# A decoder trunk with expert layers: two rows of scheduling constants and one more group of experts ahead of the gates

## The chip, the cores and the metric

The kernel runs on one core of a Trainium2 chip. The metric is the device time of one execution in microseconds (us), the median of several runs. Beside it there is one execution taken with the hardware profiler. The engines are called as in the profile: PE (TensorE, matrix multiply), DVE (VectorE), ACT (ScalarE), POOL (GpSimd), SP (SyncE, which here only issues transfers). Each works through its own instructions in their order and waits for the others by semaphores. The 16 DMA engines are shared by all queues.

## The reference, cut to what matters

Two layers, each a sequence mixer and then a PEER expert layer; 512 tokens of width 1024, float32. The expert layer is what the change concerns:

```
def block(xt):                                  # PEER, per token t and head h (8 heads)
    q = (xt @ w_q).reshape(T, 8, 2, 128)
    s = einsum('thpd,hpkd->thpk', q, sub_keys)  # scores against 2 x 128 keys
    s_top, i_top = top_k(s, 16)
    cand, cand_id = all sums of the two halves, i0 * 128 + i1
    best, pos = top_k(cand, 16); eid = cand_id[pos]; gate = softmax(best)
    act = gelu(einsum('td,thkd->thk', xt, u_tab[eid]))
    return einsum('thk,thkd->td', gate * act, v_tab[eid])
```

There are 16384 experts, each a row of `u_tab` and of `v_tab`; a token uses 8 x 16 = 128 of them.

## The kernel before

Products are in three float32r passes: an operand is split into a high part (ACT, `hi`, L172) and a low part (DVE, `lo`, L173). `stream` loads 128 x 1024 floats (512 KB, `raw`, five buffers, SP's queue) and splits them into one of six pairs of buffers. A block of 128 experts needs its `u` block for the first product (24 matmuls, L188 to L190, into `pA` or `pC`) and its `v` block for the second (18 matmuls, L1137).

An expert layer has these stages:

- *Routing* (`route_topk`). The query projection comes in four chunks of two heads. For each chunk `c` and each block `tb` of 128 tokens, `steps` finds the top 16 of four key sets on DVE, one set a step (L867 to L871); `choose` combines the halves, for the first 128 tokens chunk by chunk, for the others at the end.
- *The first 64 tokens* take their `u` rows by gather. When a chunk's experts are chosen, ACT copies the indices (`ids`, L91), POOL issues 16 gathers (`urow`, L744, eight buffers), and DVE takes 16 dots (L108), whose place among the steps is set by `DOTS[c][tb]`. After them `weigh` multiplies the gates by GELU of the dots; then POOL issues 32 adds (`gz<-gate`, L130) of gate weights into the DRAM tensor `gz`, each an indirect transfer of one number for each of 128 partitions. How many adds are issued where is set by `ADDS[c]`: the first number ahead of `choose`, the second behind it, the third (chunk 0) after a later step. POOL's queue is in order, so gathers wait for the adds ahead of them. Adds of one head wait for the landing of those of the head before.
- *Gates* (`route_gates`): for tokens 128 to 383, one slice of 32 tokens after another, one-hot products on PE give the dense gate weights, which go to DRAM (`gd<-gbuf`, L939).
- *Lookahead* (`lookahead`): beside routing and gates PE takes the first product of the first `NLA` groups of four blocks, for tokens 64 to 383. The results `ge` are spilled to DRAM (`sp`, L767), the last two groups stay. It is advanced by credits that routing and gates hand out; what is left when they end follows behind them.
- *Experts* (`experts`): groups in an order that spreads the "fresh" ones (not taken ahead) among the spilled ones. For each group `fetch` reads back gates (`gt<-gd`, `gt<-gz`) and `ge`; DVE and ACT make `ch` and `cl` from them, PE takes the second product, and, six blocks ahead, the first product of fresh blocks. The first group is fresh and the two after it are the kept ones. Beside it the last 128 tokens are done entirely by gather, in 128 rounds (POOL rows from u and v, L991; DVE dot L1003 and accumulation L1016), paced by `used`: a spilled block counts 1, a fresh one 2, and 140 iterations are spread over the total times 1.02.

The order on each engine is set when the kernel is built, by a scheduler with estimated times that starts from the program's order.

Of the kernel before, what the change touches and what calls it, by code (L numbers as in the profile page):

```python
# [37 lines left out]
GQ = 8  # L38
LAG = GQ + 4
NSD = TD // 32  # L40
NLA = 24
NSZ = 4
KEEP = 2
ROT = 3
# [1 line left out]
QS = 8  # L46
Y2 = 1.45
YA = 2.3
DOTS = ((0, 2, 2, 0), (0, 0, 1, 2), (1, 0, 1, 2), (1, 0, 2, 2))
ADDS = ((0, 0, 16), (4, 12), (6, 26), (0, 64))  # L50
YB = (1.4, 1.4, 1.4, 4.0)
AHEAD = 6
TAIL = 4
# [92 lines left out]
class Kern:  # L146
# [547 lines left out]
    def peer(self, layer, xT, hs, out):  # L694
        nc, tc, io = self.nc, self.tc, self.io
        gd = self.dram.tile([NG, P, NSD - NSZ, NB, 32], F32, name="gd%d" % layer, tag="gd%d" % layer)
        sp = self.dram.tile([NLA, P, NB, TN], F32, name="sp%d" % layer, tag="sp%d" % layer)
        with tc.tile_pool(name="pe", bufs=1) as pe:
# [60 lines left out]
    def lookahead(self, layer, xT, sp):  # L759
        for g in range(NLA):  # L760
            ge = self.pe.tile([P, NB, TN], F32, name="ge", tag="ge", bufs=3)
            for b in range(NB):
                self.mm1(layer, g * NB + b, xT, ge[:, b, :], b % 2 == 1)
                if g >= NLA - KEEP:
                    self.kept[g] = ge
                elif b == NB - 1:
                    self.nc.sync.dma_start(out=sp[g], in_=ge)  # L767
                yield

    def route_topk(self, layer, xT, kT, gz):  # L770
        nc, tc, io = self.nc, self.tc, self.io
        with tc.tile_pool(name="rt", bufs=1) as rt, tc.tile_pool(name="rt2", bufs=2) as rt2, \
# [72 lines left out]
            def scores(tb):  # L845
                ps = self.psB.tile([P, 512], F32, name="pB", tag="pB")
                for i in range(4):
                    nc.tensor.matmul(ps[:, i * P:(i + 1) * P], qs[i][:, tb * P:(tb + 1) * P], keys[:, i, :],
                                     start=True, stop=True)
                return ps  # L850
# [8 lines left out]
            def top16(c, tb, ps):  # L859
                ixs = rs2.tile([P, 4, 16], U32, name="ix", tag="ix", bufs=2)  # L860
                for i in range(4):
                    hp = c * 4 + i
                    sc = ps[:, i * P:(i + 1) * P]
                    mx = stop[:, tb, hp, :]
                    ix = ixs[:, i, :]
                    s2 = rs2.tile([P, P], F32, name="s2", tag="s2")
                    nc.vector.max(out=mx[:, 0:8], in_=sc)  # L867
                    nc.vector.max_index(out=ix[:, 0:8], in_max=mx[:, 0:8], in_values=sc)
                    nc.vector.match_replace(out=s2, in_to_replace=mx[:, 0:8], in_values=sc, imm_value=NEG)
                    nc.vector.max(out=mx[:, 8:16], in_=s2)  # L870
                    yield nc.vector.max_index(out=ix[:, 8:16], in_max=mx[:, 8:16], in_values=s2).ins  # L871
                nc.vector.tensor_copy(itop[:, tb, c * 4:c * 4 + 4, :], ixs)
# [3 lines left out]
            def steps(c, tb, ps, cost, early=0):  # L876
                for i, top in enumerate(top16(c, tb, ps)):
                    if early == "w" and c < 3:
                        w0.append(self.stream(wq[c + 1, i]))
                    with tc.issue_after(top):  # L880
                        gz.dots(self, DOTS[c][tb])
                    yield cost

            for c in range(4):
                yield from steps(c, 0, scores(0), YA)
                if c > 1:
                    gz.weigh(self, rs2)
                gz.add(self, ADDS[c][0])
                yield from choose(0, c * 2, 2)
                gz.add(self, ADDS[c][1])  # L890
                yield from steps(c, 1, scores(1), YA, "w")
                late = [scores(tb) for tb in (2, 3)]
                if c < 3:
                    self.w0, w0 = w0, []
                    keys = project(c + 1)
                for tb in (2, 3):
                    yield from steps(c, tb, late[tb - 2], YB[c])
                    if c == 0 and tb == 2:
                        gz.weigh(self, rs2)
                        gz.add(self, ADDS[c][2])  # L900
            gz.weigh(self, rs2)
# [117 lines left out]
    def experts(self, layer, xT, hs, gd, gz, sp, norm):  # L1019
        nc, tc, io = self.nc, self.tc, self.io  # L1020
        with tc.tile_pool(name="ex", bufs=2) as ex, tc.tile_pool(name="ga", bufs=2) as ga:
# [4 lines left out]
            rounds = self.gather_rounds(layer, (self.eid, self.gate3, self.x3, hs[3]), ga)  # L1026
            total = NLA * NB * 1.0 + (NE - NLA * NB) * 2.0
            done, used = 0, 0.0
            ges = {}
            kept = list(self.kept)  # L1030
            fresh, old = list(range(NLA, NG)), [g for g in range(NLA) if g not in kept]
            fresh = fresh[ROT:] + fresh[:ROT]
# [8 lines left out]
            def fetch(n):  # L1041
# [7 lines left out]
                q = nc.scalar if n > 1 else nc.sync  # L1049
                if g < NLA and g not in kept:  # L1050
                    q.dma_start(out=ge, in_=sp[g])
# [218 lines left out]
```

## Time and profile before

| | |
|---|---|
| median of 3 runs | 2786.56 us (2786.25 to 2786.89) |
| profiled execution | 2787.97 us, its span 2786.1 us |
| mean granted PE clock | 0.984 |
| PE busy | 2681.8 us (96%) |
| DVE busy | 2418.5 us (87%) |
| POOL busy | 1423.1 us (51%) |
| moved by DMA | 830.56 MB, mean 298 GB/s |

In layer 0 the routing with its gathers and adds runs from about 170 to 580 us of the span, the gates to 673, the experts to 1339. In layer 1 the same stages end at about 2020, 2115 and 2776. Timeline rows give start, duration, engine, line, operation, and in brackets the idle time before and what ended it. Rows of waits give the sum, the number and the longest. Rows of windows give busy time and count of PE, PE's weight loads, DVE, ACT and POOL, then the granted PE clock, the DMA share and GB/s. Single matmuls overlap: the spacing of their starts counts, not their length.

### The profile page before, as it was taken

The numbers are of one execution on the slowest core, as the hardware profiler recorded it, in microseconds if no ns is written. First come the engines' busy times: TensorE is split into PE (matmuls) and PEld (weight loads), VectorE is DVE, ScalarE is ACT, GpSimd is POOL, SyncE is SP. The second block draws the span as 40 slices with busy tenths as digits, with TensorE's granted clock in tenths as the row PEclk, the third lists the DMA queues.
The fourth block names the chain that finished last, engine by engine and source line by source line (L and its number), as shares of the span: only waits on it lengthen the run. The fifth ranks groups of instructions, "written<-read, shape, count | busy, mean of one in ns | idle before, by whom it ended". The sixth has DMA issues, their size and how long they took to land. (4 is left out here: it accounts for less than half of the span.)

```text
span 2786.1 us, 41803 instructions
## 1 busy us (share of the span) xinstructions
PE 2681.8 (96%) x15314; PEld 2375.7 (85%) x15314; DVE 2418.5 (87%) x4684; ACT 1093.1 (39%) x1539; POOL 1423.1 (51%) x929
## 2 busy tenths in 40 slices
PE   9999997998999999999999999997998999999998
PEld 7898997997887888888788899997997888888887
DVE  6678887997799999999798678897997899999999
ACT  3343332565333333333334343342654333333332
POOL 0006778781466666565000026778862556666663
PEclk9999998999999999999999999998999999999999
DMA  6357888799999999999322557888799999999995
GB/s 230 123 201 257 267 270 247 218 250 313 353 408 409 414 412 413 410 402 371 104 78 78 201 182 226 260 274 272 195 285 329 366 418 413 410 408 413 413 415 216
DMA packets 330414, 830.56 MB, mean 298 GB/s; under 512 B 63456, under 2 KB 129504, under 8 KB 330208
## 3 DMA queue, kind: packets, MB, share of 16 engines
q1 hardware_dynamic: 177248, 415.08, 42.0%
q0 software_dynamic: 129344, 336.78, 34.0%
q10 hardware_dynamic: 23616, 76.03, 6.9%
q8 instruction: 120, 1.97, 0.3%
q14 instruction: 86, 0.70, 0.1%
HBM read 746.38 MB, written 81.40 MB: 297 GB/s over the span
## 5 line engine op out<-in xcount | busy, mean ns | idle before, releaser
L172 ACT CAST hi<-raw 128x1024 fp32r<-128x1024 f32 (+1 forms) x609 | 637.8, 1051 | 1107.2 <-DMA raw<-in_peer_v 349.9
L173 DVE TENSOR_TENSOR lo<-raw,hi 128x1024 fp32r<-128x1024 f32 (+1 forms) x609 | 732.8, 1213 | 96.8 <-ACT hi L172 93.6
L190 PE MATMUL pA<-xThi,lo 128*128 128x320 f32 (+2 forms) x1712 | 560.4, 327 | 37.1 <-DVE lo L173 37.1
L991 POOL DMA_INDIRECT row<-in_v,eid x256 | 384.5, 1502 | 374.8 <-DVE av L1003 279.8
L130 POOL DMA_INDIRECT gz<-gate,idx x256 | 491.5, 1920 | 147.4 <-issue 78.9
L188 PE MATMUL pA<-xThi,hi 128*128 128x320 f32 (+2 forms) x1712 | 561.6, 328 | 0.2 <-ACT hi L172 0.2
L189 PE MATMUL pA<-xTlo,hi 128*128 128x320 f32 (+2 forms) x1712 | 559.5, 327 | 0.4 <-DVE xTlo L173 0.4
L991 POOL DMA_INDIRECT row<-in_u,eid x256 | 379.6, 1483 | 106.5 <-issue 69.5
L190 PEld LDWEIGHTS pA<-xThi,lo 128*128 128x128 f32 x1712 | 323.2, 189 | 53.1 <-DVE lo L173 38.6
L1016 DVE SCALAR_TENSOR_TENSOR h<-row,cf,h 128x1024 f32<-128x1024 f32 x256 | 327.8, 1280 | 22.3 <-DMA row<-in_v,eid 20.7
L188 PEld LDWEIGHTS pA<-xThi,hi 128*128 128x128 f32 x1712 | 323.2, 189 | 16.0 <-ACT hi L172 0.7
L189 PEld LDWEIGHTS pA<-xTlo,hi 128*128 128x128 f32 x1712 | 323.2, 189 | 16.0 <-DVE xTlo L173 0.7
L1003 DVE CUSTOM_DVE_ANT_0 row<-row,x 128x1024 f32<-128x1024 f32 x256 | 310.8, 1216 | 13.5 <-DMA row<-in_u,eid 13.1
L1137 PE MATMUL pB<-hi,ch 128*128 128x512 f32 x768 | 301.6, 393 | 20.9 <-ACT ch L1086 20.9
L1137 PE MATMUL pB<-lo,ch 128*128 128x512 f32 x768 | 303.9, 396 | 16.6 <-DVE lo L173 15.1
L1137 PE MATMUL pB<-hi,cl 128*128 128x512 f32 x768 | 301.2, 392 | 3.8 <-DVE cl L1093 3.8
L1137 PE MATMUL pC<-hi,ch 128*128 128x512 f32 x768 | 301.4, 392 | 0.0
L1137 PE MATMUL pC<-lo,ch 128*128 128x512 f32 x768 | 301.0, 392 | 0.0
L1137 PE MATMUL pC<-hi,cl 128*128 128x512 f32 x768 | 300.7, 392 | 0.0
L744 POOL DMA_INDIRECT urow<-in_u,ids x128 | 157.2, 1228 | 221.1 <-ACT ids L91 173.3
L190 PE MATMUL pC<-xThi,lo 128*128 128x320 f32 x768 | 240.0, 312 | 11.6 <-DVE lo L173 11.6
L188 PE MATMUL pC<-xThi,hi 128*128 128x320 f32 x768 | 240.8, 314 | 0.0
(280 smaller groups left out, 4571.5 us busy)
## 6 DMA issues: line engine op xcount, KB each, us to landing
raw<-in_peer_ut SPq DMA_DIRECT2D x256, 512.0 KB
raw<-in_peer_v SPq DMA_DIRECT2D x256, 512.0 KB
gd<-gbuf SPq DMA_DIRECT2D x16, 2048.0 KB
gt<-gd ACTq DMA_DIRECT2D x60, 512.0 KB
sp<-ge SPq DMA_DIRECT2D x44, 640.0 KB
ge<-sp ACTq DMA_DIRECT2D x44, 640.0 KB
raw<-in_peer_w_q SPq DMA_DIRECT2D x32, 512.0 KB
gz<-zero SPq DMA_DIRECT2D x64, 256.0 KB
```

What stands on the lines that cost most here:

```text
L130: d = nc.gpsimd.indirect_dma_start(out=flat, out_offset=bass.IndirectOffsetOnAxis(ap=self.idx[c][:, col], axis=0), in_=gate[:, col], in_of ...
L172: self.nc.scalar.copy(hi, src)
L173: return self.nc.vector.tensor_tensor(lo, src, hi.bitcast(F32), ALU.subtract)
L188: nc.tensor.matmul(ps, ah, bh, start=(first and i == 0), stop=False)
L189: nc.tensor.matmul(ps, ah, bl, start=False, stop=False)
L190: nc.tensor.matmul(ps, al, bh, start=False, stop=(last and i == n - 1))
L744: d = self.nc.gpsimd.indirect_dma_start(out=t, out_offset=None, in_=self.io["u%d" % layer], in_offset=bass.IndirectOffsetOnAxis(ap=ids[:, ...
L991: nc.gpsimd.indirect_dma_start(out=t, out_offset=None, in_=io[name], in_offset=bass.IndirectOffsetOnAxis(ap=at, axis=0))
L1003: dot = nc.vector.tensor_tensor_reduce(ur, ur, x, 1.0, 0.0, ALU.mult, ALU.add, av[:, k:k + 1])
L1016: nc.vector.scalar_tensor_tensor(acc, vr, c, acc, ALU.mult, ALU.add)
L1137: nc.tensor.matmul(acc[hf], a[:, ts], b[:, hf * 512:(hf + 1) * 512], start=first and i == 0, stop=last and i == 2)
```

## The change

Three constants and the indexing of one of them; the arithmetic and the number of instructions of each kind of work stay, but for one more group spilled and read back in each layer. `DOTS` now has a number for each of the four steps, the same as before except for chunk 0, whose 16 dots are 0, 1, 2, 2 and then 3, 3, 3, 2 instead of 2 in each of eight steps. `ADDS` moves adds: 18 instead of 20 ahead of the second chunk's gathers, 14 instead of 18 between the second's and the third's, 17 instead of 26 between the third's and the fourth's, and 79 instead of 64 behind the fourth's. `NLA` goes from 24 to 25 groups.

```diff
-NLA = 24
+NLA = 25
...
-DOTS = ((0, 2, 2, 0), (0, 0, 1, 2), (1, 0, 1, 2), (1, 0, 2, 2))
-ADDS = ((0, 0, 16), (4, 12), (6, 26), (0, 64))
+DOTS = (((0,) * 4, (0, 1, 2, 2), (3, 3, 3, 2), (0,) * 4), ((0,) * 4, (0,) * 4, (1,) * 4, (2,) * 4),
+        ((1,) * 4, (0,) * 4, (1,) * 4, (2,) * 4), ((1,) * 4, (0,) * 4, (2,) * 4, (2,) * 4))
+ADDS = ((0, 0, 16), (2, 14), (0, 17), (0, 128))
...
-                        gz.dots(self, DOTS[c][tb])
+                        gz.dots(self, DOTS[c][tb][i])
```

Line numbers behind the constants are one higher after the change.

The first place is POOL's queue in layer 0, from the adds of chunk 0 on (`gate_1408` to `gate_1411` are the gates of the four chunks; `urow` are a chunk's 16 gathers in four rows). Before:

```order
L130 DMA gz_1418<-gate_1408,idx_1412 2097152x1 x20
...
L744 DMA urow_2759<-in_u,ids 128x1024
L130 DMA gz_1418<-gate_1408,idx_1412 2097152x1 x12
L130 DMA gz_1418<-gate_1409,idx_1413 2097152x1 x6
...
L744 DMA urow_3587<-in_u,ids 128x1024
L130 DMA gz_1418<-gate_1409,idx_1413 2097152x1 x26
...
L744 DMA urow_4390<-in_u,ids 128x1024
L130 DMA gz_1418<-gate_1410,idx_1414 2097152x1 x32
L130 DMA gz_1418<-gate_1411,idx_1415 2097152x1 x32
```

And after the change:

```order
L131 DMA gz_1418<-gate_1408,idx_1412 2097152x1 x18
...
L745 DMA urow_2757<-in_u,ids 128x1024
L131 DMA gz_1418<-gate_1408,idx_1412 2097152x1 x14
...
L745 DMA urow_3581<-in_u,ids 128x1024
L131 DMA gz_1418<-gate_1409,idx_1413 2097152x1 x17
...
L745 DMA urow_4375<-in_u,ids 128x1024
L131 DMA gz_1418<-gate_1409,idx_1413 2097152x1 x15
L131 DMA gz_1418<-gate_1410,idx_1414 2097152x1 x32
L131 DMA gz_1418<-gate_1411,idx_1415 2097152x1 x32
```

Between the third and the fourth chunk's gathers 17 adds are left of 26, and 15 adds of the second chunk now follow the last gathers, ahead of the 64.

The second place is DVE in layer 0 at the first chunk's dots (two rows L108 a dot; the `lo` row is a split of a streamed block). Before:

```order
L173 TENSOR_TENSOR lo<-raw,hi 128x1024
L108 ISA urow,avu<-urow,xx 128x1024
L108 ISA avu 128x1
L108 ISA urow,avu<-urow,xx 128x1024
L108 ISA avu 128x1
L870 MAX stop<-s_2116 128x8
L173 TENSOR_TENSOR lo<-raw,hi 128x1024
L108 ISA urow,avu<-urow,xx 128x1024
L108 ISA avu 128x1
L108 ISA urow,avu<-urow,xx 128x1024
L108 ISA avu 128x1
L871 MAX_INDEX ix<-stop,s_2116 128x8
```

And after:

```order
L174 TENSOR_TENSOR lo<-raw,hi 128x1024
L109 ISA urow,avu<-urow,xx 128x1024
L109 ISA avu 128x1
L109 ISA urow,avu<-urow,xx 128x1024
L109 ISA avu 128x1
L871 MAX stop<-s_2113 128x8
L174 TENSOR_TENSOR lo<-raw,hi 128x1024
L109 ISA urow,avu<-urow,xx 128x1024
L109 ISA avu 128x1
L872 MAX_INDEX ix<-stop,s_2113 128x8
L109 ISA urow,avu<-urow,xx 128x1024
L109 ISA avu 128x1
```

The first two dots and the split behind them stand where they stood; from the fourth dot on they come later.

The third place is SP's queue at the end of the gates in layer 0 (`gd<-gbuf` writes a gate slice, `sp<-ge` spills a group, `gt<-gd` reads the first gates back). Before:

```order
L767 DMA sp_1025<-ge 128x1280
L178 DMA raw<-in_peer_ut 128x1024
L178 DMA raw<-in_peer_v 128x1024
L939 DMA gd_1024<-gbuf 128x32x128
L178 DMA raw<-in_peer_v 128x1024 x2
L939 DMA gd_1024<-gbuf 128x32x128
L178 DMA raw<-in_peer_v 128x1024 x2
L939 DMA gd_1024<-gbuf 128x32x128
L178 DMA raw<-in_peer_v 128x1024
L178 DMA raw<-in_peer_ut 128x1024
L939 DMA gd_1024<-gbuf 128x32x128
```

And after:

```order
L179 DMA raw<-in_peer_ut 128x1024 x2
L940 DMA gd_1024<-gbuf 128x32x128
L768 DMA sp_1025<-ge 128x1280
L179 DMA raw<-in_peer_ut 128x1024
L179 DMA raw<-in_peer_v 128x1024
L940 DMA gd_1024<-gbuf 128x32x128
L179 DMA raw<-in_peer_v 128x1024 x2
L940 DMA gd_1024<-gbuf 128x32x128
L179 DMA raw<-in_peer_v 128x1024 x2
L1054 DMA gt<-gd_1024 128x1024 x2
```

Four more `u` blocks are loaded ahead of the first `v` block, so that two gate writes instead of four come behind it. On PE 167 matmuls of the first product stand between the last gate product and the first of the second product, instead of 71: seven blocks instead of three.

## The prediction

> **What bounds the kernel now.** I read the engines' shares first, then who waits for whom on the TensorE (PE), then the time order around its long waits, then the stage windows.
>
> ```profile
> PE 2681.8 (96%) x15314; PEld 2375.7 (85%) x15314; DVE 2418.5 (87%) x4684; ACT 1093.1 (39%) x1539; POOL 1423.1 (51%) x929
> PE pA L190 <- DVE lo L173: 37.1, 6, 17.9
> PE pB L1137 <- ACT ch L1086: 20.9, 2, 10.8
> PE pB L1137 <- DVE lo L173: 15.1, 13, 3.6
> PE pC L190 <- DVE lo L173: 11.6, 4, 4.8
> DVE urow L108 <- DMA urow<-in_u,ids: 76.4, 19, 17.7
> ```
>
> PE is the bound: 96% busy, and nearly all of its idle time is in its four rows here; the fifth is DVE's wait behind two of them. So the change is worth what it takes from them and from the slow clock behind them, less what it adds. Each sits at one place per layer.
>
> **The long wait (37.1 us): the fourth chunk's gathers.** Rows of layer 0 in order of time, then of layer 1; the last two are windows (PE, PEld, DVE, ACT, POOL busy, granted clock, DMA share, GB/s).
>
> ```profile
> 392.63 2.63 POOL L130 DMA_INDIRECT gz<-gate,idx  x1 [0.30 <-issue]
> 427.99 0.42 ACT L91 COPY ids<-eu 64x16 int32<-64x16 int32 x2 [0.30 <-DVE s L869]
> 437.26 0.28 DVE L871 FIND_INDEX8 ix<-stop,s 128x8 uint32<-128x128 f32 x1
> 449.06 1.55 POOL L130 DMA_INDIRECT gz<-gate,idx  x1 [0.30 <-issue]
> 450.91 1.00 POOL L744 DMA_INDIRECT urow<-in_u,ids  x1 [0.30 <-issue]
> 455.15 1.23 DVE L108 CUSTOM_DVE_ANT_0 urow<-urow,xx 128x1024 f32<-128x1024 f32 x1 [17.61 <-DMA urow<-in_u,ids]
> 470.80 0.63 PE L190 MATMUL pA<-xThi,lo 128*128 128x320 f32 x1 [17.94 <-DVE lo L173]
> 1870.61 0.42 ACT L91 COPY ids<-eu 64x16 int32<-64x16 int32 x2 [0.30 <-DVE eu L89]
> 1893.54 1.00 POOL L744 DMA_INDIRECT urow<-in_u,ids  x1 [0.30 <-issue]
> 1897.86 1.23 DVE L108 CUSTOM_DVE_ANT_0 urow<-urow,xx 128x1024 f32<-128x1024 f32 x1 [17.70 <-DMA urow<-in_u,ids]
> 455.00:470.00 15.00, 0.00 (x0) 0.00 (x0) 13.65 (x44) 0.00 (x0) 12.26 (x10) 0.51 0.95 339
> 470.00:480.00 10.00, 9.20 (x47) 9.21 (x48) 10.00 (x28) 1.31 (x2) 8.21 (x6) 0.71 0.94 347
> ```
>
> The indices are ready at 428.4, but POOL works through 26 adds (392.63 to 450.6, 2.23 us each) and starts the gathers 22.5 us later. DVE comes to the first dot at 437.5, stands 17.6 us, and the splits queued behind it (lo, L173) starve PE. Then PE runs at half clock for some us.
>
> **The other waits.** First the earlier chunks, with the first chunk's dots last; then the start of the expert stage.
>
> ```profile
> 356.35 0.42 ACT L91 COPY ids<-eu 64x16 int32<-64x16 int32 x2 [0.30 <-DVE s L869]
> 367.29 1.00 POOL L744 DMA_INDIRECT urow<-in_u,ids  x1 [0.30 <-issue]
> 371.47 1.22 DVE L108 CUSTOM_DVE_ANT_0 urow<-urow,xx 128x1024 f32<-128x1024 f32 x1 [7.84 <-DMA urow<-in_u,ids]
> 301.30 1.23 DVE L108 CUSTOM_DVE_ANT_0 urow<-urow,xx 128x1024 f32<-128x1024 f32 x1 [4.19 <-DMA urow<-in_u,ids]
> 217.60 1.22 DVE L108 CUSTOM_DVE_ANT_0 urow<-urow,xx 128x1024 f32<-128x1024 f32 x1 [2.78 <-DMA urow<-in_u,ids]
> 220.91 1.23 DVE L108 CUSTOM_DVE_ANT_0 urow<-urow,xx 128x1024 f32<-128x1024 f32 x1 [2.07 <-DMA urow<-in_u,ids]
> 223.53 0.64 PE L190 MATMUL pC<-xThi,lo 128*128 128x320 f32 x1 [4.79 <-DVE lo L173]
> 674.01 0.38 SPq L939 DMA_DIRECT2D gd<-gbuf  x1
> 684.55 0.80 SPq L1053 DMA_DIRECT2D gt<-gd  x2
> 694.48 0.79 PE L1137 MATMUL pB<-hi,ch 128*128 128x512 f32 x1 [10.81 <-ACT ch L1086]
> 698.61 0.79 PE L1137 MATMUL pB<-hi,cl 128*128 128x512 f32 x1 [2.06 <-DVE cl L1093]
> 2136.20 0.80 PE L1137 MATMUL pB<-hi,ch 128*128 128x512 f32 x1 [10.06 <-ACT ch L1086]
> 694.00:705.00 11.00, 8.46 (x20) 6.21 (x21) 8.49 (x14) 2.20 (x4) 5.04 (x4) 0.52 1.02 419
> ```
>
> At the start of the experts the last gate slice goes to DRAM at 674.0, has landed at 684.5, is read back, weighed and split; PE, out of blocks at 683.7, idles 10.8 us and crawls at clock 0.52 until 705. Last, the expert stage itself: single matmuls for their spacing, and two windows.
>
> ```profile
> 782.04 0.40 PE L1137 MATMUL pC<-hi,ch 128*128 128x512 f32 x1
> 786.13 0.39 PE L1137 MATMUL pC<-hi,ch 128*128 128x512 f32 x1
> 822.11 0.30 PE L188 MATMUL pA<-xThi,hi 128*128 128x320 f32 x1
> 824.31 0.31 PE L188 MATMUL pA<-xThi,hi 128*128 128x320 f32 x1
> 960.00:1060.00 100.00, 98.65 (x465) 82.79 (x464) 94.33 (x112) 34.37 (x40) 63.25 (x42) 1.00 1.02 412
> 684.00:1320.00 636.00, 615.05 (x2904) 519.63 (x2905) 577.87 (x677) 218.87 (x261) 383.81 (x258) 0.98 1.01 401
> ```
>
> 18 matmuls of 512 columns take 4.09 us, so 0.227 each and 4.09 a block of the second product; 15 of 320 columns take 2.20, so 0.147 each and 3.52 a block of the first. The DMA engines are full (share 1.02 at 412 GB/s): PE and DMA are both at their limit here, and 15.1 us of PE waits (two layers) are the DMA's share.
>
> **The parts and their costs.**
>
> *Fewer adds ahead of the gathers.* Six adds go from before the third chunk's gathers to behind them, and fifteen stand behind the fourth chunk's 16 gathers that stood before; two move behind the second chunk's. Layer 0 on POOL: the second chunk's gathers start some 3.7 us sooner (two adds of 1.85, the step from 449.06 to 450.91), which covers nearly all of the 4.19; the third's at the indices, 356.8 instead of 367.3, so that data lands near 361 and the dot wanted at 363.6 (371.47 less 7.84) does not wait. The 16 gathers took 25 us, so the 17 adds run from about 383 at 2.23, to 421, with the wait between two heads perhaps 424. That is ahead of 428.4, so the fourth chunk's gathers start at the indices, land 4.2 us later (450.91 to 455.15), at 433, and DVE comes at 437.5: no stall, 4 us to spare. In layer 1 the indices are ready at 1871.0 and DVE comes at 1880.2 (1897.86 less 17.70).
> PE gains the 17.94 and the slow clock (470 to 480: 47 matmuls where 10/0.147 = 68 fit, 3.1 us), 21 us. DVE's order at this place is unchanged: eight dots and four top-16 searches still stand between two splits, and PE's stock runs out about when the next split now comes, so I leave 1 us: 20 us a layer, 40 in all. The smaller waits on earlier chunks (11.6 less 4.79 here and about as much in layer 1: 2.2) go too: **42 us**.
> Who pays: 79 adds now follow the last gathers instead of 64. The gathers end 24.0 us after they start (450.91 to 474.89), now at 452; by the two rows at the slower rival an add takes 2.44 us with waits, and 452 + 79 x 2.44 is 645. They must have been issued by 658 (there). Covered, at nothing.
>
> *First chunk's dots later.* On DVE the first two dots stand where they stood (they wait 2.78 and 2.07), and the split behind them, which PE waits for, keeps its place. Only the dots after it move, where PE waits for nothing. Gain 0; bounds -2 (later splits sooner) to +2 (three dots in a row) for both layers.
>
> *25 groups.* Four u blocks a layer go ahead: 4 x 3.52 = 14.1 us of PE work in the hole, with their splits and GELUs, which idle DVE and ACT take. On SP four u loads go ahead of the v loads; the read of gt waits for the landing as before. By 705 PE had done 20 matmuls of the second product; now it ends the blocks at 683.7 + 14.1 = 697.8 and runs on at full clock, 32 by 705: 14.1 + 12 x 0.227 = 16.8 us ahead (layer 1, whose wait is 0.75 shorter, 16). One more group is spilled (SP's queue) and read back (ACT's), 0.66 MB each way, written where PE isn't waiting for DMA.
> But the expert stage loses 14.1 us of PE time and hardly any bytes. A block of a spilled group needs v 0.524, a quarter of gt and ge 0.360, and 140/(160 x 1.02) = 0.858 gather rounds of 1.049 MB: 1.784 MB in 4.09 us, 436 GB/s. A fresh block: 3.045 MB in 7.61 us, 400. A period of 4 fresh and 12.6 spilled blocks: 34.6 MB, 84.0 us at 412 GB/s against 81.9 of PE, 2.1 us over, seven times. Now rounds are 0.880, and a period has 15.3 spilled blocks: 40.1 MB, 97.3 us against 93.2, 4.1 over, six times. The stage pays 24.6 instead of 14.7, **10 us a layer** of the 16. Ends: nothing given back (33 gained in all), everything (0). I take 16.8 + 16 - 20 = **13 us**, since the share 1.02 stands in nearly every window.
>
> The Trainium skill (DMA: Bandwidth & Descriptors, Specifications) puts the ceiling of the 16 DMA engines at 435 GB/s and the HBM's share of one core at about 358. The trace holds 412 over 100 us, so the lower figure does not bind here, and no window shows the upper. By 435 a new period takes 92 us, under PE's 93.2, nothing is given back, and the sum would be 75 us.
>
> Sum: 42 + 0 + 13 = 55 us. The profiled execution took 2787.97 (span 2786.1), 1.4 above the runs' median of 2786.56; so 2733 beside the profile, **2732** as a median.
>
> **Rivals.**
> *Nothing given back* (10%): buffers carry the spilled stretches over the fresh ones. For it: PE's explicit waits there are only 7.5 us a layer. Against: share 1.02. Gain 42 + 33: 2712.
> *All given back* (10%): the expert stage is DMA's alone, and four prefetched v blocks fewer make up for the four u loads. Gain 42: 2744.
> *The gathers stay late* (7%): 17 adds hit the indices' time if they take over 45/17 = 2.65 us each instead of 2.23, for instance beside the denser traffic. At 3.2 they are 9 us late a layer: about 2750.
> *Slower* (4%): the adds' tail. PE now has blocks until about 676 (gates end 21 sooner, 24.6 us of blocks behind), and from the read of gt to the second product went 14 us (684.55 to 698.61); so the last add must have landed by 662.
>
> ```profile
> 474.89 1.95 POOL L130 DMA_INDIRECT gz<-gate,idx  x1 [0.30 <-issue]
> 629.18 1.98 POOL L130 DMA_INDIRECT gz<-gate,idx  x1 [0.30 <-issue]
> ```
>
> 64 adds took 156.3 us, 2.44 each. An add takes about 4 us to land if it is like a gather (450.91 to 455.15), so 658 is the last issue. At (658 - 452)/79 = 2.61 each they begin to hold the experts; the gain is gone at 27 us a layer more, 2.95 each, and at 3.1 the kernel takes 2810. Against: the 64 already ran beside four of the eight gate slices (629.18 lies 45 us ahead of the last one's write) and kept to 2.44.
> *No change* (2%): DVE, busy throughout 455 to 480, absorbs it; but its own stall goes with PE's.
>
> **How the numbers follow.** The likeliest case has 67%, own range 2722 to 2742. The range takes in all given back and most of nothing given back, and the late gathers' edge: 2714 to 2750. A difference under 0.2%, some 5.6 us, cannot be told from none: faster 0.94, same 0.02, slower 0.04.
>
> **What would show it.** Right: DVE's waits for urow fall from 76.4 us to under 20, those of the first chunk staying; the wait of 17.9 is gone and no PE clock near 0.5 is left in the routing but for the first chunk's; PE goes from first to second product with under 2 us between. PE's waits for lo in the expert stage grow from 15 to some 35 us. Wrong: the fourth chunk's first gather later than its indices, or the read of gz later than that of gd.

## The result, and the profile after

The changed kernel takes 2747.67 us (median of 4 runs, 2743.87 to 2748.59); the kernel before, run beside it, 2786.4. The ratio is 0.986 (95% interval 0.9843 to 0.9877): 39 us faster, where 55 were forecast, 2714 to 2750 was the range and 2722 to 2742 that of the likeliest case. The profiled execution took 2748.59 (span 2746.7).

First the engines and who waits for whom, as before the change (line numbers are one higher).

```profile
PE 2679.3 (98%) x15314; PEld 2374.9 (86%) x15314; DVE 2419.7 (88%) x4684; ACT 1093.3 (40%) x1539; POOL 1427.3 (52%) x929
PE pB L1138 <- DVE lo L174: 26.9, 15, 3.2
DVE urow L109 <- DMA urow<-in_u,ids: 21.4, 18, 2.9
PE pC L191 <- DVE lo L174: 10.8, 6, 4.3
PE pB L1138 <- ACT ch L1087: 9.4, 2, 5.3
PE pA L191 <- DVE lo L174: 4.1, 7, 1.0
```

The 37.1 us behind the fourth chunk have become 4.1. The wait at the start of the experts fell only from 20.9 to 9.4, and the waits for `lo` in the expert stage grew from 15.1 to 26.9. Where in the span this lies is read from two marks in each layer: the last gate product and the last matmul of the second product (rows of lines: count, ns, first and last start). First before, then after.

```profile
L934 PE MATMUL pC<-og,oh x64: 217/218/220, 586.8 to 673.0; 128*128 128x128 f16 x64
L1137 PE MATMUL pC<-hi,cl x384: 388/389/628, 699.2 to 1338.9; 128*128 128x512 f32 x192
L934 PE MATMUL pC<-og,oh x64: 217/218/219, 2029.3 to 2115.5; 128*128 128x128 f16 x64
L1137 PE MATMUL pC<-hi,cl x384: 388/389/628, 2140.6 to 2775.6; 128*128 128x512 f32 x192
```

```profile
L935 PE MATMUL pC<-og,oh x64: 218/218/220, 570.7 to 656.8; 128*128 128x128 f16 x64
L1138 PE MATMUL pC<-hi,cl x384: 388/389/628, 689.2 to 1318.4; 128*128 128x512 f32 x192
L935 PE MATMUL pC<-og,oh x64: 217/218/220, 1990.1 to 2076.2; 128*128 128x128 f16 x64
L1138 PE MATMUL pC<-hi,cl x384: 387/389/632, 2107.4 to 2735.0; 128*128 128x512 f32 x192
```

Up to the gates' end the layers became 16.2 us (673.0 to 656.8) and 18.8 us shorter (2115.5 - 1338.9 = 776.6, now 757.8): 35 where the adds' term had 42. The expert stages became 4.3 (665.9 to 661.6) and 1.3 us shorter (660.1 to 658.8): 5.6 where the groups' term had 13.

**The fourth chunk.** Indices, POOL's adds and first gather, PE's waits, and a window (busy times, then clock, DMA share, GB/s), layer 0 after the change:

```profile
425.86 0.42 ACT L92 COPY ids<-eu 64x16 int32<-64x16 int32 x2 [0.30 <-DVE eu L90]
426.86 1.54 POOL L131 DMA_INDIRECT gz<-gate,idx  x1 [6.34 <-DVE iy L103]
428.71 1.71 POOL L745 DMA_INDIRECT urow<-in_u,ids  x1 [0.31 <-issue]
454.66 0.41 PE L191 MATMUL pA<-xThi,lo 128*128 128x320 f32 x1 [0.96 <-DVE lo L174]
459.27 0.41 PE L191 MATMUL pC<-xThi,lo 128*128 128x320 f32 x1 [0.82 <-DVE lo L174]
463.88 0.42 PE L191 MATMUL pA<-xThi,lo 128*128 128x320 f32 x1 [0.83 <-DVE lo L174]
455.00:480.00 25.00, 23.35 (x156) 22.59 (x155) 24.93 (x90) 7.96 (x14) 21.65 (x12) 1.00 0.98 301
```

The stall is gone and PE keeps its full clock, but the gathers start 2.4 us after the indices are copied (428.71 against 425.86 + 0.42). The 17th add is the first of its head; it stood 6.34 us, and the gathers stood behind it. The row names `iy`, which belongs to the fourth chunk's indices and which this add, one of the second chunk's, does not read. What the program makes the add wait for is the landing of the head before, and other first adds stand as long (5.80 us at 1914.29, ended by `DMA gz<-gate`). PE's waits here sum to 2.6 us.

**The start of the experts.** Last add, the reads of the gates (SP's in one row and POOL's in two are those of the first two groups), DVE's weighing and PE's first second product in layer 0, then DVE's first weighing and PE's first second product in layer 1:

```profile
661.77 2.48 POOL L131 DMA_INDIRECT gz<-gate,idx  x1 [0.30 <-issue]
669.42 0.80 SPq L1054 DMA_DIRECT2D gt<-gd  x2
670.73 0.62 POOL L142 DMA_DIRECT2D gt<-gz  x1 [6.47 <-DMA raw<-in_peer_v]
672.67 0.61 POOL L142 DMA_DIRECT2D gt<-gz  x1
682.15 0.82 DVE L1083 TENSOR_TENSOR gt<-gt,ge 128x640 f32<-128x640 f32 x1 [12.28 <-DMA raw<-in_peer_ut]
685.16 0.82 DVE L1083 TENSOR_TENSOR gt<-gt,ge 128x640 f32<-128x640 f32 x1
686.90 0.80 PE L1138 MATMUL pB<-hi,ch 128*128 128x512 f32 x1 [5.29 <-ACT ch L1087]
2100.36 0.82 DVE L1083 TENSOR_TENSOR gt<-gt,ge 128x640 f32<-128x640 f32 x1 [11.10 <-DMA gt<-gz]
2105.11 0.80 PE L1138 MATMUL pB<-hi,ch 128*128 128x512 f32 x1 [4.11 <-ACT ch L1087]
```

DVE's first weighing waits 12.28 us, then two splits run, then the second weighing, and only then does ACT make `ch`. (Layer 0's row names a streamed block as what ended the wait; layer 1's names the read of `gz`.) The first weighing began 12.7 us after the first read (669.42 to 682.15), and PE followed 4.75 us later. Before the change it began 8.2 us after that read (684.55), PE 1.75 us later:

```profile
692.73 1.62 DVE L1082 TENSOR_TENSOR gt<-gt,ge 128x640 f32<-128x640 f32 x2 [6.88 <-DMA gt<-gz]
```
DVE's order in the built program tells why (the numbers tell buffers apart): `gt_7622` holds the gates of the second group in the experts' order (one that was kept), `gt_7619` those of the first.

```
L174 TENSOR_TENSOR lo_7785<-raw_7782,hi_7784 128x1024
L1083 TENSOR_TENSOR gt_7622<-gt_7622,ge_7194 128x10x64
L174 TENSOR_TENSOR lo_7842<-raw_7839,hi_7841 128x1024
L174 TENSOR_TENSOR lo_7854<-raw_7851,hi_7853 128x1024
L1083 TENSOR_TENSOR gt_7619<-gt_7619,ge_7618 128x10x64
```

Before the change both weighings of the first group came first. With 25 groups the scheduler puts one of the kept group, whose `ge` has long been there, ahead; why it does so now was not tested. That group's gates are read second on both queues (POOL's read at 672.67 against 670.73), and DVE takes its instructions in order, so the first group's weighing stands behind a read that was queued later.

### The profile page after: what moved, and what is told of

It is laid out like the page before. It is cut to its first block, busy times and chain, and to the rows that moved or that the text cites. A ratio compares the mean times of both kernels' runs of the same rounds, so it can differ in the third digit from the quotient of the medians.

```text
span 2746.7 us, 41827 instructions
## 1 busy us (share of the span) xinstructions
PE 2679.3 (98%) x15314; PEld 2374.9 (86%) x15314; DVE 2419.7 (88%) x4684; ACT 1093.3 (40%) x1539; POOL 1427.3 (52%) x929
## 4 chain that ended last, share of the span: by engine, by line
PE 50%; DVE 15%; issue 14%; DMA 11%; POOL 8%; ACT 1%; SPq 0%; DVEq 0%; POOLq 0%; ACTq 0%
PE pA L191 9%; PE pA L190 8%; PE pA L189 8%; POOL row L992 7%; PE pB L1138 5%; DMA row<-in_v,eid 5%; PE pC L1138 5%; DVE lo L174 4%; DMA raw<-in_peer_v 3%; PE pC L191 3%; PE pC L189 3%; PE pC L190 3%; DVE h L1017 2%; DVE row L1004 2%; DMA urow<-in_u,ids 1%
## 5 line engine op out<-in xcount | busy, mean ns | idle before, releaser
L131 POOL DMA_INDIRECT gz<-gate,idx x256 | 505.7, 1975 | 165.7 <-issue 72.5
L992 POOL DMA_INDIRECT row<-in_v,eid x256 | 367.0, 1434 | 359.5 <-DVE av L1004 262.9
L191 PE MATMUL pA<-xThi,lo 128*128 128x320 f32 (+2 forms) x1680 | 548.8, 327 | 4.1 <-DVE lo L174 4.1
L189 PE MATMUL pA<-xThi,hi 128*128 128x320 f32 (+2 forms) x1680 | 550.5, 328 | 0.8 <-ACT hi L173 0.8
L190 PE MATMUL pA<-xTlo,hi 128*128 128x320 f32 (+2 forms) x1680 | 548.1, 326 | 0.4 <-DVE xTlo L174 0.4
L992 POOL DMA_INDIRECT row<-in_u,eid x256 | 388.4, 1517 | 123.3 <-issue 68.0
L191 PEld LDWEIGHTS pA<-xThi,lo 128*128 128x128 f32 x1680 | 315.6, 188 | 20.2 <-DVE lo L174 6.0
L189 PEld LDWEIGHTS pA<-xThi,hi 128*128 128x128 f32 x1680 | 315.7, 188 | 17.2 <-ACT hi L173 2.1
L1138 PE MATMUL pB<-lo,ch 128*128 128x512 f32 x768 | 303.8, 396 | 27.4 <-DVE lo L174 26.9
L190 PEld LDWEIGHTS pA<-xTlo,hi 128*128 128x128 f32 x1680 | 315.8, 188 | 15.8 <-DVE xTlo L174 0.7
L191 PE MATMUL pC<-xThi,lo 128*128 128x320 f32 x800 | 250.5, 313 | 10.8 <-DVE lo L174 10.8
L189 PE MATMUL pC<-xThi,hi 128*128 128x320 f32 x800 | 251.2, 314 | 0.0
```

The source lines that it names most:

```text
L131: d = nc.gpsimd.indirect_dma_start(out=flat, out_offset=bass.IndirectOffsetOnAxis(ap=self.idx[c][:, col], axis=0), in_=gate[:, col], in_of ...
L189: nc.tensor.matmul(ps, ah, bh, start=(first and i == 0), stop=False)
L190: nc.tensor.matmul(ps, ah, bl, start=False, stop=False)
L191: nc.tensor.matmul(ps, al, bh, start=False, stop=(last and i == n - 1))
L992: nc.gpsimd.indirect_dma_start(out=t, out_offset=None, in_=io[name], in_offset=bass.IndirectOffsetOnAxis(ap=at, axis=0))
L1138: nc.tensor.matmul(acc[hf], a[:, ts], b[:, hf * 512:(hf + 1) * 512], start=first and i == 0, stop=last and i == 2)
```

## The experiments

Each kernel ran beside the kernel before; the medians of that differ a little (2785.7, 2783.3 and 2784.1 us in three series), so gains are given against it. Ratios have 95% intervals.

| run | time, us | ratio | gain, us |
|---|---|---|---|
| the change | 2747.67 | 0.986 (0.9843 to 0.9877) | 38.7 |
| adds_only | 2749.85 | 0.9871 (0.9856 to 0.9886) | 35.9 |
| groups_only | 2780.45 | 0.9987 (0.9978 to 0.9996) | 5.3 |
| dots_only | 2783.83 | 0.9992 (0.9983 to 1.0001) | 1.9 |
| first_group_first | 2734.89 | 0.9818 (0.9804 to 0.9832) | 50.8 |
| less_dve | 2725.23 | 0.9798 (0.9783 to 0.9813) | 58.0 |
| less_bytes | 2690.82 | 0.9668 (0.9653 to 0.9682) | 92.5 |
| sixteen_adds | 2729.69 | 0.9805 (0.9791 to 0.9818) | 53.6 |
| groups_26 | 2755.36 | 0.99 (0.9884 to 0.9915) | 27.9 |
| late_adds | 2762.14 | 0.9919 (0.9902 to 0.9936) | 22.0 |

**The three parts alone.** Edits: one constant of the diff each (`ADDS`; `NLA`; `DOTS` with its index).

> The new row of adds alone, with 24 groups and the old dots. Theory (the adds carry nearly all): by the two traces the routing and gates became 16.2 + 18.7 us shorter, so about 2751. Rival (the prediction's terms, 42 for the adds and 13 for the groups, with a common loss elsewhere): 2744 to 2747, and taking the 25th group back would cost nothing or gain. In both the gap at the start of the experts stays at 10 us or more a layer, and the gate slices' way to it shows whether the adds' tail (79 adds at 2.6 us) now ends last: then the gap grows by some us.

> 25 groups alone, with the old adds and dots; no tail of adds near the experts' start. Theory (DVE weighs the second group's gates ahead of the first's, and the expert stage gives back about 7 us a layer): the start still waits 4 to 5 us a layer, 5 to 6 us gained, about 2781. Rival 1 (the adds' tail, which this kernel lacks, held the start in the changed kernel): no wait at the start, 2773 or lower. Rival 2 (all given back): 2786.

> The first chunk's new dots alone. Theory: nothing, 2786 within 2 us; the wait of PE behind the first dots falls by about 0.4 us a layer as in the changed kernel. Rival: PE's slow clock behind it lasts twice as long (6.8 instead of 3.4 us in layer 0 of the changed kernel) because of the new dots, a loss of 2 us.

The adds alone gain 35.9 us, the groups 5.3, the dots nothing that can be told from none (the interval reaches 1.0001). The three sum to 43.1 against 38.7 together, and the intervals are too wide to say whether the parts overlap. All three times are near those of the first theory. Two details are not: the wait behind the first chunk's dots fell by 0.4 us in one layer of dots_only (4.79 to 4.42) but rose by 0.3 in the other (4.60 to 4.91), and the split by stage is not clean, since adds_only's expert stages are 3.3 us shorter too (661.9 and 660.8 us against 665.9 and 660.1). PE's first wait for the experts, adds_only ahead and groups_only behind:

```profile
679.55 0.80 PE L1137 MATMUL pB<-hi,ch 128*128 128x512 f32 x1 [10.77 <-DMA gt<-gz]
2097.73 0.80 PE L1137 MATMUL pB<-hi,ch 128*128 128x512 f32 x1 [9.96 <-ACT ch L1086]
```

```profile
700.56 0.80 PE L1137 MATMUL pB<-hi,ch 128*128 128x512 f32 x1 [3.66 <-ACT ch L1086]
2136.22 0.61 PE L1137 MATMUL pB<-hi,ch 128*128 128x512 f32 x1 [3.12 <-ACT ch L1086]
PE pB L1137 <- DVE lo L173: 26.8, 14, 3.1
```

groups_only has the old, early adds and still waits 3.7 and 3.1 us, so in it the adds' tail is not what holds the start; and it has the grown waits in the expert stage (26.8; 12.7 in adds_only), so these belong to the groups. Its DVE order has the kept group ahead as well; adds_only's has not.

**The first group first.** The weighing returns its instruction, and the second group's is issued after both of the first group's:

```diff
-                    nc.vector.tensor_tensor(gf, gf, ge[...], ALU.mult)
+                    m = nc.vector.tensor_tensor(gf, gf, ge[...], ALU.mult)
...
+                return m
...
-                high(i, None)
+                turn = high(i, None)
```

> The changed kernel, with DVE's weighing of the second group's gates put behind both weighings of the first group's. Theory: the first weighing no longer stands behind a read that is queued later, the second product starts 5 us sooner a layer, the waits of 5.3 and 4.1 us and the slow clock behind them go (12 us in all), of which the full DMA takes back a third to a half: 2739 to 2742. Rival 1 (the first group's own gates land no sooner): 2747 and the same waits. Rival 2 (all given back in the expert stage): 2747, without the waits at the start.

It gained 12.1 us more than the change (50.8 against 38.7). Its timeline in layer 0: the read of the first group's gates on SP, POOL's, and DVE's weighing; below them windows at the start of both layers' experts.

```profile
672.03 0.80 SPq L1054 DMA_DIRECT2D gt<-gd  x2
673.02 0.62 POOL L142 DMA_DIRECT2D gt<-gz  x1 [7.65 <-DMA raw<-in_peer_v]
679.87 0.82 DVE L1083 TENSOR_TENSOR gt<-gt,ge 128x640 f32<-128x640 f32 x1
682.00:697.00 15.00, 15.00 (x75) 12.87 (x74) 11.94 (x17) 6.74 (x8) 6.09 (x6) 1.00 1.03 420
2093.00:2110.00 17.00, 17.00 (x89) 14.98 (x88) 13.90 (x19) 8.01 (x10) 7.89 (x6) 1.00 1.03 418
```

The weighing starts 7.8 us after the read, without a wait of its own; PE passes from the first to the second product without a gap and at full clock, in both layers. So the order on DVE caused the 9.4 us and the slow clock behind them. More was kept than expected: nothing of these 12 us came back as waits in the expert stage (24.0 us for `lo` now, 26.9 before), though PE's waits at layer 0's fourth chunk were longer in this run (4.9 us against 2.6).

**What takes time back in the expert stage.** DVE is busy 94 of 100 us there and the DMA share is over 1; either could make `lo` late. Two kernels cut one and then the other, on the base of the run before. less_dve leaves out half of the columns that DVE accumulates; less_bytes leaves out, besides, half of each row of v that is gathered.

```diff
-                nc.vector.scalar_tensor_tensor(acc, vr, c, acc, ALU.mult, ALU.add)
+                nc.vector.scalar_tensor_tensor(acc[:, :512], vr[:, :512], c, acc[:, :512], ALU.mult, ALU.add)
```

and, for less_bytes, besides that

```diff
+            if name[0] == "v":
+                src, dst = src.rearrange("r (two c) -> (r two) c", two=2), t[:, :512]
```

> The kernel with the first group first, and in the 128 gather rounds of a layer DVE accumulates only half of the 1024 columns (the other half is left out of the output): some 0.6 us less of DVE a round, 80 us a layer, the bytes unchanged. Theory (the expert stage gives time back because the DMA engines are full): the 24 us of PE's waits for lo stay, 2735 within 4. Rival (DVE, busy 94 of 100 us there, is the late one): the waits go, 2715 to 2720.

> The same, and the rows of v gathered in those rounds are half as long (which halves are read is not the reference's): 33 MB a layer less of some 250, the DVE work as in the run before it. Theory (DMA): PE's waits for lo in the expert stage fall from 24 us to under 6, with their slow clock some 15 to 25 us less than the run before it: 2712 to 2720. Rival (DVE): the same time as the run before it.

Windows of 500 us within each layer's expert stage: the base, less_dve, less_bytes, with the waits of the last two.

```profile
760.00:1260.00 500.00, 489.74 (x2297) 414.82 (x2296) 469.55 (x550) 171.40 (x203) 312.80 (x212) 0.99 1.02 413
2180.00:2680.00 500.00, 486.00 (x2286) 410.26 (x2285) 469.90 (x550) 171.30 (x204) 315.64 (x212) 0.99 1.02 413
```

```profile
760.00:1260.00 500.00, 486.81 (x2301) 412.27 (x2300) 419.04 (x556) 171.99 (x206) 270.41 (x214) 1.00 1.02 414
2180.00:2680.00 500.00, 488.87 (x2298) 414.34 (x2297) 419.14 (x553) 172.88 (x206) 277.93 (x211) 0.99 1.02 413
PE pB L1139 <- DVE lo L174: 24.2, 13, 3.8
```

```profile
760.00:1260.00 500.00, 500.00 (x2377) 426.00 (x2376) 432.98 (x573) 180.94 (x213) 296.25 (x218) 1.00 0.97 368
2180.00:2680.00 500.00, 500.00 (x2376) 425.92 (x2375) 428.29 (x572) 174.04 (x208) 276.51 (x205) 1.00 0.92 348
```

With DVE down from 470 to 419 of 500 us PE's waits stay (24.0 and 24.2) and its work in the windows hardly grows (2297 to 2301 matmuls and 2286 to 2298). With fewer bytes PE is busy all 500 us, the row of waits for `lo` in the second product is gone, and 76 and 78 more matmuls pass. So in these windows it is the bytes and not DVE's work that make `lo` late; whether the DMA engines or the memory behind them set the limit, these runs do not separate. less_bytes gained 34.5 us on less_dve, more than the 15 to 25 expected. less_dve gained 7.2 on its base where nothing beyond 4 was expected, so DVE's work is not quite free: in the profiled executions its expert stages are 6.2 and 2.9 us shorter. A part of this lies at the end of layer 0's experts, where in a window of 57 us the DMA share is down to 0.7 and PE got 251 instead of 236 matmuls done (base, then less_dve); the rest was not located.

```profile
1260.00:1317.00 57.00, 53.42 (x236) 43.53 (x236) 53.82 (x66) 19.52 (x24) 13.16 (x9) 0.97 0.66 239
1250.90:1307.90 57.00, 55.42 (x251) 45.18 (x250) 54.09 (x77) 19.81 (x25) 18.23 (x12) 1.00 0.70 267
```

The Trainium skill (DMA: Bandwidth & Descriptors, Specifications) gives about 358 GB/s as the HBM's share of one core and 435 as the ceiling of the fabric that the 16 engines share. The full windows hold 413 to 414, so with one core at work the first does not bind, and the second is not reached: PE already waits at 413.

**26 groups.** Edit: `NLA = 26`, on the base of first_group_first.

> The kernel with the first group first, and 26 groups. Theory (the hole at the start is filled by 25, and each group more only takes PE work without bytes out of the full expert stage): 2 to 8 us a layer are given back and nothing is gained, 2738 to 2750. Rival (nothing is given back): 2735.

It gained 22.9 us less than 25 groups, beyond the expected 3 to 15. The start had no hole left to fill, and PE's waits for `lo` grew to 35.6 us in 23 places (24.0 in 11). From the last gate product to the last second product a layer took 7.9 and 9.5 us longer, so of the 28 us of first product moved ahead of the experts only some 11 came off them (an estimate from these differences).

**The adds.** Edits on the same base: `(0, 16)` and `(0, 8)` for `(0, 17)` in the row of `ADDS`.

> The kernel with the first group first, and 16 instead of 17 adds between the third and the fourth chunk's gathers, in place of the add that is the first of its head and stood 6.1 to 6.8 us for the landing of the head before. Theory: the fourth chunk's gathers start at their indices, 2 to 5 us sooner, DVE's waits there shrink and PE's (4.9 us in layer 0, 1.7 in layer 1) halve: 2730 to 2733. Rival (DVE's own eight dots between two splits make these waits): 2735.

> The kernel with the first group first, and 8 instead of 17 adds between the third and the fourth chunk's gathers, so that 88 instead of 79 follow the last gathers. In the kernel it starts from the last add of layer 0 was issued at 663.8 and the first read of gz at 673.0, with no wait of PE. Theory (the prediction's slower rival: the adds' tail ends last at 2.64 us an add): the last add comes 9 x 2.64 = 24 us later, less 3 to 5 us by which the gathers start sooner, so the first read of gz about 18 us later a layer; with the slow clock behind such a wait 35 to 45 us slower, 2770 to 2780. Rival (the adds' place is hidden with room to spare): 2730 to 2735.

With 16 the gathers follow the indices at once (they wait for `ids`, no longer for an add), first row; it gained 2.8 us on its base, by two gains whose intervals overlap, so the size is not sure. PE's waits for `lo` into `pA` are 1.5 us in it, against 3.4 to 6.1 in the six kernels with this row of adds. With 8, the next rows, the last add is issued at 683.2 and the first read of gz at 687.5; PE stands 14.7 and 14.6 us in the two layers, because ACT, which issues a read of `gz` too, waits for the same adds and does no split or GELU behind it until 686.8.

```profile
426.65 1.00 POOL L745 DMA_INDIRECT urow<-in_u,ids  x1 [6.03 <-ACT ids L92]
```

```profile
683.22 1.56 POOL L131 DMA_INDIRECT gz<-gate,idx  x1 [0.30 <-issue]
687.46 0.62 POOL L142 DMA_DIRECT2D gt<-gz  x1 [2.69 <-issue]
689.17 0.63 PE L189 MATMUL pA<-xThi,hi 128*128 128x320 f32 x1 [14.74 <-ACT ge L758]
2119.42 0.64 PE L189 MATMUL pA<-xThi,hi 128*128 128x320 f32 x1 [14.58 <-ACT ge L758]
```

The kernel lost 28.8 us against its base (35 to 45 expected): nine more adds behind the gathers bring the waiting for the adds' tail of which the slower rival speaks. sixteen_adds, at 0.9805, is the fastest of the kernels that leave nothing out.

## Why the prediction was right, and where it was off

The sign and the place held, and the time lies in the range, 2.3 us from its upper end and outside the likeliest case's own; the sum was 16 us too large. Of the signs named, DVE's waits for `urow` fell to 21.4 us instead of under 20, PE's waits for `lo` in the expert stage grew to 26.9 instead of some 35, and PE did not pass from the first to the second product with under 2 us between.

- *Fewer adds: 42 forecast, 35 in the profile, 35.9 by adds_only.* The mechanism is as told. Mis-sized were the sub-terms. PE's waits at the place, allowed for with 1 us a layer, are 2.6 and 2.3, so 2.9 more. The step that had the 17 adds end at 424 allowed some 3 us for the wait between two heads; it took 6.34, the adds began 2.4 us later than forecast (385.44), and the 17th ended at 428.4, behind the indices; sixteen_adds bears this out. The slow clock was priced at 3.1 us a layer from the matmuls between 470 and 480, but PE starts at 470.80, so 0.8 us of the wait was counted twice. The granted clock after the stall gives (1 - 0.75) x 10.2 = 2.6 and (1 - 0.86) x 10.2 = 1.4, so 2.2 less in all. Of the smaller waits, forecast at 2.2, 1.6 went (0.88 to 0.35 and 1.34 to 0.32). The last 1.2 us were not located.

```profile
470.80:481.00 10.20, 10.20 (x54) 10.20 (x55) 10.20 (x28) 1.38 (x2) 8.68 (x6) 0.75 0.97 343
1913.30:1923.50 10.20, 9.59 (x54) 9.33 (x55) 10.20 (x28) 1.38 (x2) 8.68 (x6) 0.86 0.95 355
```

- *First chunk's dots: 0 forecast*, 1.9 measured, not told from 0. Right.
- *25 groups: 13 forecast, 5.6 in the profile, 5.3 alone.* The step that failed is "runs on at full clock" from 697.8, which took the weighing and its order on DVE as they were. That order changed and PE stood 5.3 and 4.1 us; the prediction compared SP's and PE's orders at this place and not DVE's. Once the order is mended the term is 15 (first_group_first against adds_only in one series, 2749.85 - 2734.89, with the dots in it).
- *Given back: 20 forecast.* Start losses in adds_only were 25.8 us of waits (10.77 and 1.86, 9.96 and 3.23) and 8.0 of slow clock (0.77 and 0.71 over the 15.5 and 15.3 us behind the first ones), 33.8; first_group_first has none, and is 15 us faster, so 18.8 came back. This estimate is an upper bound: the stretches of slow clock hold the 1.86 and 3.23, which are counted partly twice. The reason, a stage at the limit of its bytes, is shown by less_bytes. By the same count the start cost 33.9 us before the change (waits of 10.81 and 2.06, 10.06 and 1.69; 0.68 and 0.71 over 15.5 and 14.8 us) and 13.6 after it (9.4 of waits, and the clock of the last section): 20.3 gained there where 32.8 were forecast, and with 5.6 left in all some 14.7 came back instead of 20. The two errors partly cancel, so the term is nearer to the forecast than its parts are. The forecast that PE's waits for `lo` there would reach 35 us was too high for 25 groups (26.9) and came true with 26 (35.6).
- *Adds' tail, "covered, at nothing".* No run shows that it cost anything here. 79 adds took 206.1 us from first to last issue (455.7 to 661.8), 2.64 each instead of 2.44. By the slower rival they begin to hold the experts at 2.61 and with a last issue after 658; that limit was too early, since first_group_first issued its last add at 663.8 and has no wait at the start. In layer 0 the read of `gz` came 1.3 us after that of `gd`, the sign named for a wrong step, but this sign tells nothing: before the change it came 1.1 us after it (685.63 and 684.55), when POOL had stood idle for 54 us. late_adds, with the last issue at 683.2, shows the cost; the edge lies somewhere between.

```profile
L131 POOL DMA_INDIRECT gz<-gate,idx x79: 1545/1976/5781, 455.7 to 661.8; - x79
```

- *Rivals.* "All given back" (2744) gives nearly the measured time and is partly right: by the estimate some 14.7 of the 20.3 us gained at the start came back. But the adds fell short as well, and the 5.3 us of PE's wait in layer 0 and 4.1 in layer 1 come from DVE's order, of which it says nothing. "The gathers stay late" happened in small (2.4 us, not 9).

## What to carry to other kernels

When a change shifts work at a place where engines meet, compare the order of every engine that stands between the wait and its release; here the one instruction that moved stood on DVE, between two engines whose orders had been compared. A hole filled with work taken from a stage that is full on DMA pays only for the part by which the hole shrinks: with DVE's order mended 25 groups closed it, and a 26th cost 23 us. A count of instructions ahead of a queue's next job is best cut where a dependency begins, not one behind it.

## What the runs showed that was not expected

Whether a wait slows PE behind it went by its length. Waits of 0.8 to 1.0 us at the fourth chunk left the granted clock at 1.00, and so did one of 2.32 us there in adds_only (455.9 to 470); the 5.3 and 4.1 us at the experts' start were followed by 0.89 and 0.83 over 15 us, and groups_only's 3.66 and 3.12 by 0.81 and 0.89 over 15.5 and 15.8:

```profile
686.90:702.00 15.10, 15.10 (x60) 12.36 (x61) 13.88 (x20) 8.01 (x10) 6.57 (x4) 0.89 0.97 370
2105.10:2120.00 14.90, 14.89 (x55) 12.12 (x56) 13.69 (x20) 6.92 (x9) 6.37 (x4) 0.83 0.96 371
```

The Trainium skill (TensorE: Matmul & The Clock Gate, Part 1) says that the clock halves after an idle window of about 3.4 us. Here the border lies between 2.3 and 3.1 us of idle time, a little below that; the ends of matmuls, from which the profile counts idle time, are modelled. In less_bytes, where no wait is left in the two windows, their clock is 1.00.
